# Two of the four weight-block sums of each seven-product pair made by DMA (a plain load and an accumulating load) in place of VectorE adds

## The chip, the cores and the metric

The kernel runs on one core of a Trainium2 chip. A core has a matrix engine (TensorE, PE in the profile, with its weight loads shown apart as PEld), a vector engine (VectorE, DVE), a scalar engine (ScalarE, ACT), a general engine (GpSimd, POOL) and a synchronisation engine (SyncE, SP). Each works through a queue of its own in order. Sixteen DMA engines move data between HBM and the on-chip memory; in this kernel SP issues nearly all transfers. The metric is the device time of one execution in microseconds (us).

## The reference

One step of a one-layer hybrid encoder over T = 544 frames: 32 frames of a running stream and 512 of a new one, model width 1024, all in fp32. The parts that matter here:

```python
xn = _rmsnorm(h, norm_g[l])
proj = xn @ w_in[l]
u, v_m, z_m, ig_pre, fg_pre, q_h, f_h, i_h, g_h, ga, gb = jnp.split(proj, _split_points(), axis=-1)
c, conv_new = _causal_conv(u, conv0, conv_w, conv_b)
c = silu(c)
# mLSTM branch: 4 heads of 512; q and k from c, v from v_m, gate z_m
hm, C_new, n_new, m_new = _mlstm(qm, km, vm, ig, lf, C0, n0, m0)
ya = ((layernorm(hm) + m_skip * c) * silu(z_m)) @ w_brm
# HGRN2 branch: 8 heads of 128, from q_h, f_h, i_h, g_h
oh, S_new = _hgrn(qh, kh, ih, lfh, S0)
yb = (rmsnorm(oh) * silu(g_h)) @ w_brh
y = sigmoid(ga) * ya + sigmoid(gb) * yb
h = h + y @ w_out
h = h + sigmoid(h @ w_pg) * (p @ w_ple)
out = _rmsnorm(h, final_g)
```

The first product, `xn @ w_in`, is the one that the change touches.

## The kernel before, in words

TensorE multiplies in a reduced fp32 form ("fp32r"). To get fp32 results, each operand is split into a high part and a low rest, and each product is made of three matmuls: high x high, high x rest, rest x high. The split of a weight piece (`split_piece`, lines 119 to 130) is a ScalarE copy into the fp32r type for the high half (line 128) and a VectorE subtraction for the low half (line 129). The halves lie in rings of five buffers each (`NPIECE`).

`w_in` is kept in units of 128 output columns; a unit is 128 x 1024 in memory, two pieces of 128 x 512 fp32 (256 KB), so (unit, 0) and (unit, 1) are the two halves of the inner dimension. A raw piece is loaded by a DMA that SP issues (`raw_piece`, lines 116 to 119; line 118 in the profile) into a ring of eight buffers (`NRAW`).

Most units are multiplied plainly (class `One`, matmuls at line 366). 52 units, as 26 pairs (a, b = a + 1), go through class `Two`, which makes the 2 x 2 block product of a pair with seven block products in place of eight. The activations' sums for this are made once for all pairs (`xf_sums`). The weights' sums are made for each pair on VectorE:

```python
s1 = (b,0) + (b,1)
s2 = s1 + (a,0)
s3 = (a,0) + (b,0)
s4 = s2 + (a,1)
```

The seven block products of a pair use the forms a11 = (a,0), s2, a12 = (a,1), s3, s1, a22 = (b,1), s4. Each form is split into halves like a raw piece and multiplied in a block of twelve matmuls of 128 x 272 (line 453). The sums lie in a ring of four buffers (`NSUM`, tag "wu"); the adds are line 418 (tiles named ws1, ws2, ws3, ws4 and the pair's number, all "ws" in a grouped row; wa1180, for example, is form a11 of pair 80, and ws284l the low half of s2 of pair 84).

Class `Pump` (lines 487 to 545) feeds these blocks. It lists all blocks of a stage by start times that are written down in `Two.blocks`: the blocks of two neighbouring pairs are interleaved, seven block times from pair to pair. `prepare` runs three blocks ahead of the one that is multiplied (`AHEAD`): it issues the raw loads, four pieces ahead (`RAWAHEAD`, line 533), and calls the block's `make`, which issues the adds and the split. `make("s2")` made s1 and s2, `make("s3")` made s3, and s4 is made with s2 or a12, whichever comes later.

The 26 pairs are used in two places. In the stages of the mLSTM heads (`fill`, lines 581 to 621), the matmuls of the pairs fill the time between the head's own work: for head 0 pairs 4 and 6, for head 1 pairs 20, 22, 36, 38, 8, 10, for head 2 pairs 24, 26, 40, 42, 12, 14, and for head 3 pairs 28, 30, 44, 46 (the numbers are those of unit a). At the end of the HGRN stage and behind it come the eight gate pairs in the order 80, 88, 82, 90, 84, 92, 86, 94; from about 927 us to 995 us of the span nothing but their blocks is multiplied. Their results pass through gate additions on VectorE (lines 474 and 476) and sigmoids on ScalarE, and then through products with the branch outputs (ya, line 1358).

The order of the instructions on PE is written out by hand. The order on VectorE, ScalarE, POOL and SP in these stages comes from a scheduler, which orders by the order of issue in the program and by the buffers that come free. POOL makes small copies and masks, and issues no DMA.

Of the kernel before, what the change touches and what calls it, by code (L numbers as in the profile page):

```python
# [9 lines left out]
F32 = mybir.dt.float32  # L10
# [4 lines left out]
ALU = mybir.AluOpType  # L15

P = 128
# [22 lines left out]
WP = 512  # L40
NRAW = 8
NSUM = 4
# [20 lines left out]
def hybrid_step(ctx: ExitStack, tc: tile.TileContext, a, o):  # L63
    nc = tc.nc
    V, S, G, PE = nc.vector, nc.scalar, nc.gpsimd, nc.tensor

    cp = ctx.enter_context(tc.tile_pool(name="cp", bufs=1))
    wp = ctx.enter_context(tc.tile_pool(name="wp", bufs=NPIECE))
# [47 lines left out]
    def raw_piece(src, name):  # L116
        raw = wp.tile([P, WP], F32, tag="wr", name=name, bufs=NRAW)
        nc.sync.dma_start(raw[:, : src.shape[-1]], src)
        return raw
# [3 lines left out]
    def split_piece(raw, name, cols=WP, chunk=WP, eng=V):  # L123
        hi = wp.tile([P, WP], F32R, tag="wh", name=name + "h")
        lo = wp.tile([P, WP], F32R, tag="wl", name=name + "l")
        for c in range(0, cols, chunk):
            c = slice(c, min(c + chunk, cols))
            high = S.copy(hi[:, c], raw[:, c])
            low = eng.tensor_tensor(lo[:, c], raw[:, c], hi[:, c].bitcast(F32), ALU.subtract)
        made[name] = high, low  # L130
        return hi, lo

    def weight(src, name, cols=1024, eng=V, chunk=WP):

        raws = [(raw_piece(src[:, c : min(c + WP, cols)], f"{name}r{c}"), min(WP, cols - c)) for c in range(0, cols, WP)]
        return [split_piece(r, f"{name}{i}", n, chunk, eng) for i, (r, n) in enumerate(raws)]
# [71 lines left out]
    def rms_cols(acc, blocks, name, pc=None):  # L208

        pc = pc or paux(name + "pc")  # L210
        n = len(blocks)
        st = small("rms_s", [P, 8])
        V.memset(st[:, :n], 1.0)
        for i, (t0, m) in enumerate(blocks):
            PE.matmul(pc[:m, 0, 2 * i : 2 * i + 2], acc[:, t0 : t0 + m], ones, start=True, stop=True)
        i = 0
        while i < n:
            j = i
            while j < n and blocks[j][1] == blocks[i][1]:
                j += 1  # L220
            m = blocks[i][1]
            V.tensor_scalar(st[:m, i:j], pc[:m, 0, 2 * i : 2 * j : 2], 1.0 / D, EPS, ALU.mult, ALU.add)
            i = j
        r = small("rms_r", [P, 8])
        rsqrt(r[:, :n], st[:, :n], P, n)
        return r
# [77 lines left out]
    def xf_sums(k):  # L304
# [20 lines left out]
        V.scalar_tensor_tensor(l[:, 3], x22, -1.0, h[:, 3].bitcast(F32), ALU.mult, ALU.subtract)  # L325
        return h, l

    xf = [None] * (KD // 2)

    class One:  # L330
# [6 lines left out]
        def raws(self):  # L337
            return [(self.unit, 0), (self.unit, 1)]

        def blocks(self, first):  # L340

            return [
                (i, [(self.unit, i // 2)] if i % 2 == 0 else [], self.prepare(i // 2) if i % 2 == 0 else None, self.run(i), {})
                for i in range(3)
            ] + [(3, [], None, self.run(3), {self.key: 1})]
# [3 lines left out]
        def prepare(self, i):  # L349
            def make(raw):  # L350
                if i == 0:
                    self.w = []
                self.w.append(split_piece(raw[self.unit, i], f"wi{self.unit}{i}"))

            return make
# [27 lines left out]
    class Two:  # L383
# [8 lines left out]

        def raws(self):
            a, b = self.unit, self.unit + 1
            return [(a, 0), (b, 0), (b, 1), (a, 1)]

        def blocks(self, first):
            a, b = self.unit, self.unit + 1
            times = (0, 3, 1, 6, 5, 9, 11) if first else (0, 3, 5, 6, 8, 9, 11)
            k = (self.what, self.f), (self.what, self.f + 1)  # L400
            return [
                (times[0], [(a, 0)], self.make("a11"), self.run("a11", 0, True, self.after1), {}),
                (times[1], [(b, 0), (b, 1)], self.make("s2"), self.run("s2", 0, False, self.after6), {}),
                (times[2], [(a, 1)], self.make("a12"), self.run("a12", 1, True, self.after2), {}),
                (times[3], [], self.make("s3"), self.run("s3", 0, False, self.after7), {}),
                (times[4], [], self.make("s1"), self.run("s1", 1, True, self.after5), {}),
                (times[5], [], self.make("a22"), self.run("a22", 0, False, self.after4), {k[1]: 1}),
                (times[6], [], self.make("s4"), self.run("s4", 1, False, self.after3), {k[0]: 1}),
            ]

        def make(self, form):
            def go(raw):
                a, b = self.unit, self.unit + 1
                q = self.sums

                def add(name, x, y):
                    q[name] = wp.tile([P, WP], F32, tag="wu", name=f"w{name}{a}", bufs=NSUM)
                    V.tensor_tensor(q[name], x, y, ALU.add)

                if form == "s2":  # L420
                    add("s1", raw[b, 0], raw[b, 1])
                    add("s2", q["s1"], raw[a, 0])
                if form == "s3":
                    add("s3", raw[a, 0], raw[b, 0])
                plain_ = {"a11": (a, 0), "a12": (a, 1), "a22": (b, 1)}
                self.w[form] = split_piece(raw[plain_[form]] if form in plain_ else q[form], f"w{form}{a}")
                if form in ("s2", "a12") and "s2" in self.w and "a12" in self.w:
                    add("s4", q["s2"], raw[a, 1])

            return go  # L430
# [77 lines left out]
    class Pump:  # L508
# [18 lines left out]
        def prepare(self, upto):  # L527
            while self.made < min(upto, len(self.order)):
                b = self.order[self.made]
                if b[1]:  # L530
                    need = self.loads.index(b[1][-1]) + 1
                    for u, i in self.loads[self.loaded : need + RAWAHEAD]:
                        self.raw[u, i] = raw_piece(a["w_in"][u][:, i * WP : (i + 1) * WP], f"wi{u}r{i}")
                    self.loaded = max(self.loaded, min(need + RAWAHEAD, len(self.loads)))
                if b[2]:
                    with tc.issue_after(self.behind.ins) if self.behind is not None else nullcontext():
                        b[2](self.raw)
                self.made += 1
# [573 lines left out]
    with tc.manual_schedule(engines={mybir.EngineType.Activation, mybir.EngineType.DVE, mybir.EngineType.PE}):  # L1112
# [15 lines left out]
        for k in range(KD):  # L1128
# [18 lines left out]
            if k in (5, 6):  # L1147
                i, j = ((0, 2), (4, 5))[k - 5]
# [8 lines left out]
        r = rms_cols(sq[0][:, :T], [(0, NS)] + [(NS + b * P, P) for b in range(NB)], "r0", pc)  # L1157
# [410 lines left out]
    for f in range(KD):  # L1568
        w = weight(a["w_brh"][f], f"wbh{f}")
# [10 lines left out]
    for f in range(KD):  # L1580
        t = slot(f"h1{f}")
        nc.sync.dma_start(t[:, :T], a["xT"][f, :, :T])
        w = weight(a["w_out"][f], f"wo{f}")
# [46 lines left out]
    with tc.manual_schedule(engines={mybir.EngineType.PE}):  # L1630
# [6 lines left out]
        for f in range(KD):  # L1637
            pg_unit(1, f)
            if f == 1:
                r = rms_cols(squares[0], blocks, "r10")  # L1640
# [5 lines left out]
        r = rms_cols(squares[1], blocks, "r11")  # L1646
# [93 lines left out]
```

## Time and profile before

| | |
|---|---|
| Time, three runs | 1174.88, 1176.25, 1178.36 us; median 1176.25 |
| The profiled execution's own time | 1176.21 us |
| Its span in the profile | 1174.5 us |
| PE busy | 1160.7 us |
| DVE busy | 883.7 us |
| ACT busy | 615.0 us |
| POOL busy | 142.3 us |
| Read from HBM | 109.32 MB |

How to read it: the span is the time from the first to the last recorded instruction of one execution; the execution's own time has some 1.7 us more around it. The busy time of an engine is the time in which it worked on an instruction; issuing a DMA and waiting don't count. A row of a timeline has the start in us, the duration in us, the engine, the line of the kernel, the operation, the tile written, the tiles read, their shape and type, and how many instructions the row joins; in square brackets stands the idle time just before it and what ended that. In a row of waits stand the waiting engine and line, what it waited for, the total in us, how often, and the longest. In a row of DMA issues the last number is the median time in us from the issue to the landing. A tile's name is shown without its buffer number in grouped rows.

### The profile page before, as it was taken

The page shows a single profiled execution, that of the slowest core. Times are in us where ns is not written, and L with a number is a line of the kernel's source. Part 1 is how long each engine was busy: PE and PEld are TensorE (multiplying, and loading weights), DVE is VectorE, ACT ScalarE, POOL GpSimd, SP SyncE. Part 2 cuts the span into 40 slices and gives each one's busy share as a digit, 9 for nine tenths or more (in the row PEclk, how much of TensorE's full clock was granted, in tenths as well). Part 3 has the DMA queues.
Part 4 walks back from the last instruction along what each step waited for, and adds up shares of the span by engine and source line. Part 5 has one row for each costly group of instructions (what it writes and reads, how often), then busy time and mean ns, then how long its engine had stood idle before and what let it go on. Part 6 is the DMA issues. An engine that isn't in the chain of part 4 may idle for free.

```text
span 1174.5 us, 24294 instructions
## 1 busy us (share of the span) xinstructions
PE 1160.7 (99%) x9089; PEld 1130.7 (96%) x9089; DVE 883.7 (75%) x2156; ACT 615.0 (52%) x1357; POOL 142.3 (12%) x283
## 2 busy tenths in 40 slices
PE   9989999999999999999999999999999999999998
PEld 8989999999999999999999999999999999999998
DVE  6976988576896768967885677877788998654485
ACT  5676557654665556665572343443433666433462
POOL 4933001100111000211000101111101100000000
PEclk9999999999999999999999999999999999999999
DMA  6133315332353233542637222222122273332753
GB/s 230 62 92 121 100 46 165 102 109 100 121 175 119 71 128 113 169 141 98 216 100 243 64 69 63 70 62 71 55 70 63 75 241 99 105 100 77 240 165 113
DMA packets 77902, 135.82 MB, mean 116 GB/s; under 512 B 8788, under 2 KB 16340, under 8 KB 77784
## 3 DMA queue, kind: packets, MB, share of 16 engines
q1 hardware_dynamic: 77616, 134.21, 35.5%
q8 instruction: 71, 1.16, 0.4%
q14 instruction: 47, 0.39, 0.1%
q10 hardware_dynamic: 168, 0.06, 0.0%
HBM read 109.32 MB, written 24.91 MB: 114 GB/s over the span
## 4 chain that ended last, share of the span: by engine, by line
PE 86%; DVE 3%; ACT 1%; issue 1%; ACTq 0%; DVEq 0%
PE d L453 22%; PE d L366 18%; PE ya L149 8%; PE pg L1599 4%; PE yb L149 4%; PE o L149 4%; PE C L833 4%; PE q L149 3%; PE k L149 3%; PE pl L1395 2%; PE nm L1003 2%; PE sc L793 2%; PE ple L149 1%; PE nm L980 1%; PE ht L1461 1%
## 5 line engine op out<-in xcount | busy, mean ns | idle before, releaser
L1387 ACT COPY km<-hk 128x256 f32<-128x256 f32 x56 | 24.0, 429 | 82.1 <-DVE hk L1413 60.1
L569 DVE SCALAR_TENSOR_TENSOR cv<-ub,vec,cv 128x547 f32<-128x547 f32 x48 | 40.4, 842 | 1.3 <-ACT cv L564 0.7
L1395 PE MATMUL pl<-hq,km 128*128 128x128 f32 x224 | 36.0, 284 | 0.0
L1413 DVE TENSOR_TENSOR hq<-hq,q 128x128 f32<-128x128 f32 (+1 forms) x96 | 25.3, 293 | 9.5 <-PE pl L1395 8.4
L933 DVE SCALAR_TENSOR_TENSOR c<-c,wi,Cs 128x258 f32<-128x258 f32 x32 | 15.3, 479 | 21.8 <-PE Cs L931 21.8
L1395 PEld LDWEIGHTS pl<-hq,km 128*128 128x128 f32 x224 | 30.8, 190 | 0.0
L467 ACT COPY t<-d 128x272 f32<-128x272 f32 x78 | 29.5, 378 | 1.2 <-PE d L453 1.0
L1449 POOL TENSOR_TENSOR at<-at,tri 32x32 f32<-32x32 f32 x8 | 3.8, 473 | 208.8 <-DVE at L1420 208.8
L1071 DVE TENSOR_TENSOR y<-ya,y 128x272 f32<-128x272 f32 x48 | 18.9, 436 | 10.7 <-PE ya L149 10.1
L1413 DVE TENSOR_TENSOR hk<-hk,q 128x128 f32<-128x128 f32 x96 | 26.2, 286 | 0.3 <-ACT km L1387 0.2
L845 ACT COPY Co<-C 128x258 f32<-128x258 f32 x32 | 10.4, 378 | 29.2 <-PE C L833 22.4
L1418 DVE COPY_PREDICATED at<-lmask,pl 128x256 f32<-128x256 uint8 x56 | 24.8, 443 | 0.0
L1509 ACT ACTIVATE osq<-kq 128x128 f32<-128x128 f32 x32 | 10.0, 311 | 25.7 <-DVE kq L1503 25.0
L1337 POOL TENSOR_TENSOR kq<-q,hk 128x544 f32<-128x544 f32 x8 | 13.9, 1739 | 61.3 <-DVE q L1335 58.5
L1014 ACT COPY y<-nm 128x516 f32<-128x516 f32 x16 | 9.4, 589 | 21.7 <-PE nm L1003 21.7
L562 POOL COPY uo<-ub 128x3 f32<-128x3 f32 x16 | 11.5, 716 | 71.3 <-DVE ub L474 50.0
L833 PE MATMUL C<-vl,kwh 128*128 128x258 f32 x96 | 19.4, 283 | 0.0
L833 PE MATMUL C<-vh,kwl 128*128 128x258 f32 x96 | 19.4, 284 | 0.0
L833 PE MATMUL C<-vh,kwh 128*128 128x258 f32 x96 | 19.4, 284 | 0.0
L963 DVE BATCH_NORM_STATS2 bs<-y 128x6 f32<-128x512 f32 (+1 forms) x20 | 13.8, 690 | 6.4 <-ACT y L1014 6.2
L731 POOL COPY vsm<-vt 128x96 f32<-128x96 f32 x16 | 7.0, 444 | 87.2 <-ACT vt L478 44.0
L807 ACT CAST sh<-dm 128x512 fp32r<-128x512 f32 (+3 forms) x16 | 7.4, 460 | 19.0 <-DVE dm L801 17.4
(4086 smaller groups left out, 4881.5 us busy)
## 6 DMA issues: line engine op xcount, KB each, us to landing
ya_d<-y SPq DMA_DIRECT2D x32, 272.0 KB, 2.2
y<-ya_d SPq DMA_DIRECT2D x24, 272.0 KB, 4.4
c<-in_C SPq DMA_DIRECT2D x16, 258.0 KB, 3.9
out_Cp<-Co SPq DMA_DIRECT2D x16, 258.0 KB, 2.7
out_Cs<-c SPq DMA_DIRECT2D x16, 258.0 KB, 2.4
x<-in_xT SPq DMA_DIRECT2D x8, 272.5 KB, 4.7
ya<-ya_d SPq DMA_DIRECT2D x8, 272.0 KB, 4.1
h<-in_xT SPq DMA_DIRECT2D x8, 272.0 KB, 4.0
```

The lines of the kernel that those rows point to most:

```text
L149: PE.matmul(both[b][:m, :TH], part(w, off + k * step, m, x), xx[:, half(b)], start=(k == 0 and j == 0), stop=(k == n - 1 and j == 2),)
L366: PE.matmul(self.ps[b][:, : c.stop - c.start], part(self.w, k * P, P, x), xx[:, c], start=(k == 0 and j == 0), stop=(k == KD - 1 and j == 2),)
L453: PE.matmul(ps, ww[:, c], xx, start=(start and k == 0 and j == 0), stop=end, skip_group_check=not start,)
L467: S.copy(t, ps)
L569: V.scalar_tensor_tensor(cv[:, :547], ub[:, j : j + 547], vcol(V_CW + 4 * ft + j), cv[:, :547], ALU.mult, ALU.add)
L793: PE.matmul(pn[:, 0, :n], ks[f][x][:, j * P : (j + 1) * P], qs[f][y][:, NS + j * P : T], start=(f == 0 and i == 0), stop=(f == KH - 1 and ...
L833: PE.matmul(pn[g][:, :VH], kw[b][x][:, f * P : (f + 1) * P], vv[b][y][:, g * VH : (g + 1) * VH], start=(b == 0 and j == 0), stop=(b == NB ...
L1387: S.copy(km.rearrange("p (n j c) -> p n j c", j=2, c=c), view(kk, HB, ((2 * c, NA // (2 * c)), (c - HB, 2), (1, c))),)
L1395: PE.matmul(pn[:, 0, b * P : (b + 1) * P], km[:, b * P : (b + 1) * P], view(qq, b * P, ((2 * c, P // (2 * c)), (HB + c, 2), (1, c))), star ...
L1413: V.tensor_tensor(xv[:, :, i, :], xv[:, :, i, :], t[:, :, 1 - i : 2 - i].to_broadcast([P, m, c]), ALU.mult)
L1418: V.copy_predicated(at[:, :NA], lmask[:, li, :NA], pn[:, 0, :NA])
L1599: PE.matmul(ps, part(w, k * P, P, x), xx[:, c], start=(k == 0 and j == 0), stop=(k == KD - 1 and j == 2))
```

## The change

Of the four sums of each pair, s1 and s3 are no longer added by VectorE. When the pair's first form (a11) is prepared, two sum buffers are taken. Into each of them SP issues a plain load of the piece (b,0); then GpSimd issues a DMA that reads the second piece from HBM, (b,1) for s1 and (a,0) for s3, and adds it to what lies in the buffer (`accum_op=ALU.add`). The piece (b,0) is no longer loaded as a raw piece, since no other form uses it, so a pair has three raw loads in place of four. The sums s2 and s4 stay on VectorE. The order of the blocks on PE is the same.

```diff
+    w_in = a["w_in"]
...
         def raws(self):
             a, b = self.unit, self.unit + 1
-            return [(a, 0), (b, 0), (b, 1), (a, 1)]
+            return [(a, 0), (b, 1), (a, 1)]
...
-                (times[1], [(b, 0), (b, 1)], self.make("s2"), self.run("s2", 0, False, self.after6), {}),
+                (times[1], [(b, 1)], self.make("s2"), self.run("s2", 0, False, self.after6), {}),
...
+                if form == "a11":
+                    for name, u, i in (("s1", b, 1), ("s3", a, 0)):
+                        q[name] = wp.tile([P, WP], F32, tag="wu", name=f"w{name}{a}", bufs=NSUM)
+                        nc.sync.dma_start(q[name], w_in[b][:, :WP])
+                        G.dma_start(q[name], w_in[u][:, i * WP : (i + 1) * WP], accum_op=ALU.add)
                 if form == "s2":
-                    add("s1", raw[b, 0], raw[b, 1])
                     add("s2", q["s1"], raw[a, 0])
-                if form == "s3":
-                    add("s3", raw[a, 0], raw[b, 0])
```

In the changed kernel the lines behind the new ones stand three further down: the plain load of a sum is line 424, the accumulating one 425, the adds 419, the matmuls 456.

More of the change, by code (lines that the diff above doesn't have):

```diff
@@ L532, in prepare @@
                     for u, i in self.loads[self.loaded : need + RAWAHEAD]:
-                        self.raw[u, i] = raw_piece(a["w_in"][u][:, i * WP : (i + 1) * WP], f"wi{u}r{i}")
+                        self.raw[u, i] = raw_piece(w_in[u][:, i * WP : (i + 1) * WP], f"wi{u}r{i}")
                     self.loaded = max(self.loaded, min(need + RAWAHEAD, len(self.loads)))
```

## The prediction

> **What bounds the kernel now.** I read the page first (span, busy times, the chain), then the waits of TensorE, then the windows of the stages that use the changed code.
>
> ```profile
> span 1174.5 us, 24294 instructions
> PE 1160.7 (99%) x9089; PEld 1130.7 (96%) x9089; DVE 883.7 (75%) x2156; ACT 615.0 (52%) x1357; POOL 142.3 (12%) x283
> PE 86%; DVE 3%; ACT 1%; issue 1%; ACTq 0%; DVEq 0%
> ```
>
> PE is busy for 1160.7 of 1174.5 us. All idle time of PE together is 13.8 us, so no relief of another engine can bring more than that. What part of it is VectorE's? The waits of PE, longest first, and the windows around the two places where a weight split is late:
>
> ```profile
> engine line waited for: us in total, times, longest us
> PE d L366 <- ACT wi320h L128: 3.3, 1, 3.3
> PE d L453 <- DVE ws210l L129: 0.4, 1, 0.4
> PE d L453 <- DVE ws214l L129: 0.4, 1, 0.4
> ```
>
> ```profile
> 312.00:334.00 22.00, 21.44 (x163) 20.18 (x162) 20.68 (x41) 14.49 (x31) 5.61 (x7) 1.00 0.43 121
> 463.00:485.00 22.00, 21.45 (x163) 20.18 (x162) 20.63 (x41) 14.43 (x31) 5.61 (x7) 1.00 0.43 129
> 940.00:995.00 55.00, 55.00 (x438) 54.79 (x437) 46.89 (x79) 34.44 (x70) 0.00 (x0) 1.00 0.53 172
> ```
>
> The columns of a window are its length, then PE, PEld, DVE, ACT and POOL busy, the clock, the DMA share and GB/s. Around ws210l and ws214l PE lacks 0.56 and 0.55 us; in the last stretch of pairs (940 to 995) it lacks nothing, DVE works 46.89 of 55 us beside it, and POOL is empty. The chain shows that stretch as one piece of matmuls:
>
> ```profile
> 927.58 12.27 PE d L453 x96
> 940.45 54.37 PE d L453 x431
> ```
>
> Here a pair takes seven blocks of twelve matmuls in 10.55 us (the starts of the same block of two pairs, 945.02 and 955.58 below, are 10.56 apart), and everything that feeds it must keep that pace.
>
> **The change, part by part.** (1) *52 adds leave VectorE.* First and last row of the 26 pairs' adds:
>
> ```profile
> L418 DVE TENSOR_TENSOR ws<-ws,wi4r x2: 687/690/692, 107.5 to 109.9; 128x512 f32<-128x512 f32 x2
> L418 DVE TENSOR_TENSOR ws<-ws,wi88r x2: 683/688/693, 901.0 to 911.3; 128x512 f32<-128x512 f32 x2
> ```
>
> 52 x 0.69 = 35.9 us less of DVE, 883.7 to about 848. On the path lies only what PE waits for: 0.56 + 0.55 us in the two windows and some tenths elsewhere, at most 1.6 us, my estimate. I take 1.0 us of gain, bounds 0 and 1.6.
>
> (2) *Each of those sums becomes a chain.* A plain load goes out on SP into one of the four "wu" buffers, then POOL issues the accumulating load into the same buffer, and only then can VectorE add s2 or ScalarE copy the high half. The chain starts when the buffer is free. In the changed program, s1 of a pair takes the buffer that the s2 of the pair before leaves, and it is free when that pair's s4 has been added. The prices that the trace has:
>
> ```profile
> 924.68 0.33 SPq L118 DMA_DIRECT2D wi90r<-in_w_in  x1
> wi92r<-in_w_in SPq DMA_DIRECT2D x2, 256.0 KB, 3.0
> wi8r<-in_w_in SPq DMA_DIRECT2D x2, 256.0 KB, 2.5
> xh<-kv_d SPq DMA_DIRECT2D x4, 256.0 KB, 6.2
> L1337 POOL TENSOR_TENSOR kq<-q,hk 128x544 f32<-128x544 f32 x8 | 13.9, 1739 | 61.3 <-DVE q L1335 58.5 <-issue 2.8
> L129 POOL TENSOR_TENSOR wk001l<-wk00r,wk001h 128x512 fp32r<-128x512 f32 x1 | 2.4, 2354 | 0.0
> ```
>
> SP issue 0.33 (0.4 with its wake), plain load of 256 KB 3.0 us. No transfer in this trace is issued by POOL and none accumulates, so the second step is bounded: at least the quickest plain load, 2.5 us; at most the slowest transfer of this size, 6.2, behind a POOL instruction of 2.4, 8.6 us. It is nearest to a weight load of 3.0 with one POOL instruction of 1.7 ahead of it and a wake like SP's: I take 5.0. The chain is L = 0.4 + 3.0 + 5.0 = 8.4 us, bounds 5.9 and 12.
>
> A rule bears on the second step. The Trainium skill, "DMA: Bandwidth & Descriptors", section "Anatomy of one DMA — SWDGE (gpsimd) path", fits a GpSimd-issued DMA as 2.0 us plus its bytes at 436 GB/s; for 256 KB that is an estimate of 2.6 us, and L would be 6.0. The section speaks of no accumulation, and no run here shows either; by it neither the tail nor the heads below would lose anything and the sum would be 1175.2 (rival A).
>
> (3) *The tail, 927 to 995 us.* The rows that pace it:
>
> ```profile
> 930.56 0.69 DVE L129 TENSOR_TENSOR ws488l<-ws,ws488h 128x512 fp32r<-128x512 f32 x1 [0.97 <-ACT ws488h L128]
> 936.08 0.69 DVE L129 TENSOR_TENSOR ws182l<-ws,ws182h 128x512 fp32r<-128x512 f32 x1
> 945.01 0.69 DVE L418 TENSOR_TENSOR ws<-ws,wi84r 128x512 f32<-128x512 f32 x1
> 947.43 0.69 DVE L129 TENSOR_TENSOR ws190l<-ws,ws190h 128x512 fp32r<-128x512 f32 x1
> 950.91 0.68 DVE L129 TENSOR_TENSOR ws284l<-ws,ws284h 128x512 fp32r<-128x512 f32 x1
> 959.55 0.68 DVE L129 TENSOR_TENSOR wa2284l<-wi85r,wa2284h 128x512 fp32r<-128x512 f32 x1
> 968.53 0.68 DVE L129 TENSOR_TENSOR ws192l<-ws,ws192h 128x512 fp32r<-128x512 f32 x1
> 978.95 0.69 DVE L129 TENSOR_TENSOR ws186l<-ws,ws186h 128x512 fp32r<-128x512 f32 x1 [0.80 <-ACT ws186h L128]
> 981.96 0.69 DVE L129 TENSOR_TENSOR ws294l<-ws,ws294h 128x512 fp32r<-128x512 f32 x1
> ```
>
> ```profile
> 945.02 0.28 PE L453 MATMUL d<-xfh,ws290h 128*128 128x272 f32 x1
> 955.58 0.28 PE L453 MATMUL d<-xfh,ws284h 128*128 128x272 f32 x1
> 987.24 0.28 PE L453 MATMUL d<-xfh,ws294h 128*128 128x272 f32 x1
> ```
>
> The halves are ready ahead of PE: ws294l ends at 982.65, PE starts it at 987.24, a lead of 4.6 us. Five chains follow one another, each for the next s2. In the changed program's VectorE order, s4 of pair 82 stands right behind ws488l, so it ends at 931.25 + 0.69 = 931.9, and s1 of pair 90 is whole L later, at 940.3, while VectorE reaches its add of s2 behind ws182l, at 936.8: 3.5 us late. VectorE is in order, so the splits and gate additions queued behind that add wait as well, and with them PE, once the lead is gone. Between that add and the end of the next s4 stand, at the pitch of these rows (0.6 for a 512-wide instruction, 0.35 for a 272-wide one, the last in full), 4.7 us of work for pair 90, 4.5 for 84, 2.9 for 92, 4.5 for 86. So s2 of pair 84 can be added at 945.0 + 8.4 = 953.4 (its place behind ws190l is 948.1: 5.3 late), 92 at 966.3 (behind wa2284l, 960.2: 6.1 late), 86 at 977.6 (behind ws192l, 969.2: 8.4 late), 94 at 990.5 (behind ws186l, 979.6: 10.9 late). Less the lead of 4.6, PE stands 6.3 us. In general the loss is 931.9 + 16.6 + 5L - 979.6 - 4.6 = 5L - 35.7: nothing up to L = 7.1, 5 us more for each us of L, 24 us at L = 12. I take 6.3, bounds 0 and 24.
>
> (4) *The head stages.* While a head of the mLSTM branch runs, two pairs follow each other closely only once, in heads 1 to 3 (pairs 36 and 38 of head 1, 40 and 42, 44 and 46):
>
> ```profile
> 245.98 0.68 DVE L129 TENSOR_TENSOR ws420l<-ws,ws420h 128x512 fp32r<-128x512 f32 x1
> 252.83 0.69 DVE L129 TENSOR_TENSOR ws122l<-ws,ws122h 128x512 fp32r<-128x512 f32 x1
> 264.28 0.69 DVE L129 TENSOR_TENSOR ws136l<-ws,ws136h 128x512 fp32r<-128x512 f32 x1 [0.80 <-ACT ws136h L128]
> 272.27 0.68 DVE L919 TENSOR_TENSOR vs<-vts,vs 32x512 fp32r<-32x512 f32 x1
> ```
>
> ```profile
> 276.98 0.28 PE L931 MATMUL Cs<-vs,kws 96*128 96x258 f32 x1
> ```
>
> In the changed order s4 of pair 22 stands behind ws420l and ends at 246.7 + 0.7 = 247.4; s1 of 36 is whole at 255.8, and the add's place is behind ws122l, at 253.5: 2.3 late. By the same count 4.5 us of work end the s4 of 36 at 260.3, s1 of 38 is whole at 268.7, and its add's place is behind ws136l, at 265.0: 3.7 late. What waits behind that add on VectorE and is wanted first is vs (ends at 272.95, PE at 276.98): a lead of 4.0, so nothing is lost at L = 8.4. The lateness is 2L - 13.1: from L = 8.6 on each head loses 2 us per us of L, 2.9 at L = 10, 6.9 at L = 12. I take 0, bounds 0 and 21. The early pairs (80, 88, 20) are loaded long before their use, covered by the HGRN matmuls and the head before; without that cover, one chain of 8.4 each.
>
> (5) *Queues and traffic.* SP issues 26 more (two plain loads for one raw load less), 26 x 0.4 = 10 us spread over the span; a plain load that waits for its buffer holds the raw loads behind it, which are issued some 10 us ahead (wi90r at 924.68, while PE starts on the pair's first sum at 945.02), so I cost it at nothing; uncovered it adds its wait to L. POOL's queue in the tail holds only these transfers. HBM reads rise by 3 x 0.26 MB x 26 = 20 MB; in 940 to 995 that is 0.79 MB per 10.55 us, 75 GB/s on 172, and the DMA share goes in proportion from 0.53 to about 0.76, which is inside the bounds of L.
>
> **Sum:** 6.3 + 0 - 1.0 = 5.3 us on the profiled execution's 1176.21 us (span 1174.5 and 1.7 around it; 0.04 under the median of the runs, 1176.25): 1181.5 us.
>
> **Rivals.** *A, the transfers are hidden.* If the accumulation takes no more than about 4.3 us, L stays under 7.7, the leads take up nearly every delay, and what is left lies between 1176.2 - 1.6 = 1174.6 and 1176.2 + 2.8 - 1.0 = 1178.0 us. For it speak the plain loads of 2.5 to 3.0 us; against it, that each sum needs two transfers one behind the other and POOL's part in the second. 0.22.
>
> *B, an accumulating transfer is far dearer*, 5.8 us or more (it must read its target as well as write it): L from 9.2, where tail and heads give 10.3 + 3.6 - 1.0 = 12.9 us; at L = 10, 14.3 + 8.7 - 1.0 = 22.0; at L = 12, 44: 1189 to 1220 us. For it speaks the 6.2 us row; against it, most weight loads at 3. 0.24.
>
> *C, POOL in order.* In the heads, POOL holds back its own work and the accumulations behind it:
>
> ```profile
> POOL vs L916 <- PE Cs L931: 94.3, 3, 34.6
> ```
>
> If accumulations that PE needs soon stand behind that wait, or small casts for PE behind an accumulation that waits for its plain load, each of three heads loses up to one L: up to 25 us, 1185 to 1207. Against it: POOL's 142.3 us of work leave it free most of the time, and a longer wait for Cs ends before the next pairs are due. 0.06.
>
> *D, the other side: VectorE's relief wins.* The late splits ws210l and ws214l and gate additions come earlier, and L stays under 7.1. It decides only where more than 3.5 us of PE's 13.8 us of idling hang on VectorE's adds; the rows above show at most 1.6. 1172. 0.05.
>
> **How the numbers follow.** The forecast, L between 7.7 and 9.2, has 0.43; its own range is 1178 to 1189, its value 1181.5. About 0.3% (3.5 us) is what a measurement of this kernel can tell from no change. Same: A's 0.22 and 0.08 of the forecast's lower end (to 1179.7). Faster: D, 0.05. Slower: 0.35 + 0.24 + 0.06 = 0.65. The range, 1175 to 1203, leaves out D, A's lowest part and the last part of B and C, about 0.18 in all.
>
> **What would show it.** Right: DVE near 848 us; PE below 55 of 55 us between 940 and its end, with waits of PE for ws2 and ws1 splits of pairs 86 and 94; VectorE idle ahead of its remaining adds, released by a POOL transfer, growing from pair 90 to 94. L can be read as the time from the plain load's issue to that add. Wrong: POOL transfers that land within 4.3 us and a full PE (A); gaps all over the heads (B or C); a gap that another engine releases.

## The result, and the profile after

| | before | after |
|---|---|---|
| Time, median of the runs | 1177.09 us (1174.88 to 1178.36) | 1213.78 us (1211.34 to 1216.3) |
| Ratio, with its 95% interval | | 1.0315 (1.0301 to 1.0328) |
| Span of the profiled execution | 1174.5 us | 1212.2 us |
| Mean granted clock over the span | 0.999 | 0.986 |

The changed kernel is 3.1% slower, about 37 us. The page of the changed kernel, first the span and the busy times, then the DMA queues and the HBM traffic, then the shares of the chain that ended last:

```profile
span 1212.2 us, 24512 instructions
PE 1172.9 (97%) x9089; PEld 1141.9 (94%) x9089; DVE 850.1 (70%) x2104; ACT 616.1 (51%) x1357; POOL 181.4 (15%) x335
...
q0 software_dynamic: 7488, 13.63, 7.2%
...
HBM read 129.77 MB, written 24.91 MB: 128 GB/s over the span
PE 84%; DVE 7%; DMA 5%; issue 2%; ACT 2%; SPq 0%; POOL 0%; DVEq 0%; ACTq 0%; POOLq 0%
```

VectorE fell from 883.7 to 850.1 us as worked out, and reads rose to 129.77 MB as worked out. But the span grew by 37.7 us, and it grew in two ways. PE's idle time went from 13.8 to 1212.2 - 1172.9 = 39.3 us (25.5 more). And the same 9089 matmuls took 1172.9 us in place of 1160.7 (12.2 more). In the chain, DMA, absent before, has 5%. (On POOL the page counts the issuing of the 52 DMAs as busy time, 45.7 of its 181.4 us.)

Where did it come from? I took the start of the same matmul in both traces; the difference is the lag at that point. The matmuls are named by their weight half:

| the same matmul | start before | lag after | since the row above |
|---|---|---|---|
| wi331h, before the heads | 116.58 | 1.9 | 1.9 |
| ws410l, end of head 1 | 332.22 | 8.3 | 6.3 |
| ws414l, end of head 2 | 483.60 | 14.1 | 5.8 |
| ws246h, end of head 3 | 589.50 | 22.3 | 8.2 |
| ws388h, start of the gate stretch | 927.51 | 23.8 | 1.6 |
| ws494h, behind the gate stretch | 996.29 | 36.9 | 13.1 |

So the heads 1 to 3 lose, some 6 to 8 us each, and the last stretch of gate pairs loses 13.1 us. The waits of the changed kernel, PE's longest, and then what VectorE waited for:

```profile
PE vt L903 <- DVE vt L477: 13.0, 3, 5.5
PE d L456 <- DVE gb L477: 7.4, 2, 4.6
...
PE d L456 <- DVE ga L477: 1.1, 1, 1.1
PE d L456 <- ACT ws210h L128: 1.1, 1, 1.1
PE d L456 <- ACT ws214h L128: 1.1, 1, 1.1
```

```profile
DVE ws L419 <- DMA ws<-in_w_in: 46.6, 13, 7.2
```

PE names VectorE, but VectorE is not busy: it stands 46.6 us in 13 places before the add of s2 until the sum's transfer has landed. What PE is short of is not weights but additions on VectorE (vt in the heads, the gate additions gb and ga in the last stretch), which stand behind that add. The waits of ws210 and ws214 did not shrink; they are 1.1 us where they were 0.4.

One link of the last stretch, in order (timeline rows of SP, POOL, DVE and PE of the changed kernel, put one under the other):

```profile
968.54 0.33 SPq L424 DMA_DIRECT2D ws<-in_w_in  x1
...
973.14 0.86 POOL L425 DMA_DIRECT2D ws<-in_w_in  x1 [10.84 <-ACT wa2290h L128]
...
979.12 0.69 DVE L419 TENSOR_TENSOR ws<-ws,wi84r 128x512 f32<-128x512 f32 x1 [7.18 <-DMA ws<-in_w_in]
...
980.68 0.43 DVE L477 TENSOR_TENSOR gb<-d,t 128x272 f32<-128x272 f32 x1
...
981.17 0.60 PE L456 MATMUL d<-xfh,ws190h 128*128 128x272 f32 x1 [4.62 <-DVE gb L477]
```

This is the sum s1 of pair 84. The plain load starts at 968.54, GpSimd issues the second transfer at 973.14, the add of s2 can start at 979.12: L is 10.6 us. VectorE idles 7.18 us ahead of the add, and the gate addition gb, three instructions behind it, lets PE go on at 981.17, after 4.62 us of idling. The windows of the stretch, from the start of ws388h to that of ws494h, and around this gap (columns as in the prediction):

```profile
951.34:1033.23 81.89, 73.38 (x547) 72.54 (x547) 51.85 (x104) 43.52 (x95) 8.59 (x10) 0.94 0.66 172
975.00:980.00 5.00, 1.55 (x13) 1.32 (x11) 0.88 (x2) 0.00 (x0) 0.87 (x1) 0.95 0.97 253
980.00:985.00 5.00, 3.83 (x17) 3.83 (x18) 4.96 (x10) 3.96 (x9) 0.00 (x0) 0.50 0.59 170
985.00:990.00 5.00, 5.00 (x37) 5.00 (x37) 2.96 (x6) 3.32 (x7) 0.89 (x2) 0.86 0.85 224
```

PE lacks 81.89 - 73.38 = 8.5 us here where it lacked nothing. Behind the gap the granted clock is 0.50 for some five us of work: 3.83 us of PE time from 980 to 985 are 17 matmuls, while 5.00 us from 985 to 990 are 37. This is the second part of the loss, and no stall shows it.

A head, the same way (head 1, pair 38; its VectorE and PE rows, then the windows around them):

```profile
272.07 0.69 DVE L419 TENSOR_TENSOR ws<-ws,wi38r 128x512 f32<-128x512 f32 x1 [5.17 <-DMA ws<-in_w_in]
272.68 0.43 DVE L477 TENSOR_TENSOR vt<-d,t 128x272 f32<-128x272 f32 x1
...
273.17 0.69 PE L903 MATMUL vt<-ident,vt 128*128 128x128 f32 x2 [3.87 <-DVE vt L477]
```

```profile
262.00:268.00 6.00, 6.00 (x51) 6.00 (x50) 4.00 (x7) 3.06 (x6) 0.21 (x1) 1.00 0.89 290
268.00:272.00 4.00, 1.30 (x12) 1.07 (x9) 0.00 (x0) 0.59 (x1) 2.69 (x10) 1.00 0.66 84
272.00:275.00 3.00, 1.83 (x8) 1.83 (x9) 2.93 (x6) 1.21 (x2) 0.00 (x0) 0.66 0.67 147
```

VectorE has no work at all from 268 to 272; 5.17 us of its waiting become 3.87 us of PE's, and the clock falls after that too (0.66).

### The profile page after: what moved, and what is told of

Read it like the earlier page. It is cut to its first block, busy times and chain, and to the rows that moved or that the text cites. A ratio compares the mean times of both kernels' runs of the same rounds, so it can differ in the third digit from the quotient of the medians.

```text
span 1212.2 us, 24512 instructions
## 1 busy us (share of the span) xinstructions
PE 1172.9 (97%) x9089; PEld 1141.9 (94%) x9089; DVE 850.1 (70%) x2104; ACT 616.1 (51%) x1357; POOL 181.4 (15%) x335
## 3 DMA queue, kind: packets, MB, share of 16 engines
q0 software_dynamic: 7488, 13.63, 7.2%
HBM read 129.77 MB, written 24.91 MB: 128 GB/s over the span
## 4 chain that ended last, share of the span: by engine, by line
PE 84%; DVE 7%; DMA 5%; issue 2%; ACT 2%; SPq 0%; POOL 0%; DVEq 0%; ACTq 0%; POOLq 0%
PE d L367 19%; PE d L456 17%; PE ya L149 8%; PE q L149 4%; PE pg L1602 4%; PE yb L149 4%; DMA ws<-in_w_in 4%; PE k L149 4%; PE o L149 4%; PE C L836 4%; PE sc L796 3%; PE pl L1398 2%; PE nm L1006 2%; PE u L269 1%; DVE cv L572 1%
## 5 line engine op out<-in xcount | busy, mean ns | idle before, releaser
L425 POOL DMA_DIRECT2D ws<-in_w_in x52 | 45.7, 879 | 244.8 <-DMA ws<-in_w_in 42.8
L903 PE MATMUL vt<-ident,vt 128*128 128x128 f32 x64 | 12.5, 318 | 13.2 <-DVE vt L477 13.0
L1512 ACT ACTIVATE osq<-kq 128x128 f32<-128x128 f32 x32 | 10.0, 311 | 26.2 <-DVE kq L1506 25.5
L753 DVE TENSOR_TENSOR kl<-kf,kh 128x512 fp32r<-128x512 f32 x16 | 11.1, 692 | 17.1 <-ACT kh L752 16.0
L903 PEld LDWEIGHTS vt<-ident,vt 128*128 128x128 f32 x64 | 8.8, 160 | 14.3 <-DVE vt L477 13.7
L1340 POOL TENSOR_TENSOR kq<-q,hk 128x544 f32<-128x544 f32 x8 | 13.9, 1742 | 45.7 <-DVE q L1338 42.9
L564 POOL COPY uo<-ub 128x3 f32<-128x3 f32 x16 | 15.3, 958 | 30.5 <-DVE ub L479 16.1
```

What stands on the lines that cost most here:

```text
L425: G.dma_start(q[name], w_in[u][:, i * WP : (i + 1) * WP], accum_op=ALU.add)
```

## The experiments

In each table row of waits or windows the line numbers are those of that kernel; all ratios are against the kernel before. The lags are read as above, at the same six matmuls. Three questions were open: is it the price of the accumulating transfer, is it the moment at which the chain may start (its buffer), or is it the added traffic?

**e1: more sum buffers in the shared ring.** The ring of sums gets six buffers, and the raw ring gives two up for the room.

```diff
-NRAW = 8
-NSUM = 4
+NRAW = 6
+NSUM = 6
```

> The changed kernel with six sum buffers in place of four, and six raw buffers in place of eight (a pair now loads three raw pieces, so two pairs still fit; the memory is the same). Theory 'start': a chain of plain load and accumulating load (7.9 to 10.7 us, read in the changed kernel's tail from the end of the s4 add to the s2 add) starts only when the s4 add of the pair before frees its buffer, VectorE waits for it in order, and PE waits for what stands behind. With two buffers more s1 and s3 of the next pair can be loaded about a pair earlier, and the waits vanish: 1176 to 1182 us, TensorE clock back at 1.00 in the tail. Rival 'traffic': 20 MB more from HBM and accumulations that take twice the engine time per MB (7.2% of 16 engines' span for 13.63 MB against 35.9% for 141.03) slow every load; the same transfers are made here, so 1205 to 1214 us.

Measured: 1214.11 us, ratio 1.0314 (1.0289 to 1.034): no gain at all. The lags are 0.0, 9.2, 17.6, 24.8, 24.2, 36.7. This seemed to speak against the start. But the number of buffers is not the time for which one is free: the sums go round one shared ring, and in this program's order the plain load for s1 of pair 84 takes the buffer of s1 of pair 82, which is free only after the split ws182l (it ends at 961.55, and the load goes out at 961.57). The experiment changed which buffer the chain waits for, and not enough how early it may begin. It decided nothing, and e5, e6 and e9 take the question up again with rings of their own.

**e2: only s1 by two transfers.** s3 goes back to VectorE, with its raw piece.

```diff
-for name, u, i in (("s1", b, 1), ("s3", a, 0)):
+for name, u, i in (("s1", b, 1),):
...
+if form == "s3":
+    add("s3", raw[a, 0], raw[b, 0])
```

> Only s1 is made by the two DMAs; s3 is again a VectorE add of (a,0) and (b,0), which is loaded as a raw piece again. Theory 'start': s1 stands on the path to s2, so nearly the whole loss stays: 1203 to 1214 us, perhaps a little less than the changed kernel since the chain shares the DMA engines with one accumulation fewer. Rival 'traffic': half of the added transfers are gone, so half of the loss: about 1195 us.

**e3: only s3 by two transfers.** The counterpart, with the add of s1 back on VectorE.

```diff
-for name, u, i in (("s1", b, 1), ("s3", a, 0)):
+for name, u, i in (("s3", a, 0),):
...
+add("s1", raw[b, 0], raw[b, 1])
```

> Only s3 is made by the two DMAs; s1 is again a VectorE add. Theory 'start': s3 is first needed three blocks (4.5 us) after s2 and nothing but its own split waits for it, so most of the loss goes: 1177 to 1186 us. Rival 'traffic': half of the added transfers are left, about 1195 us.

Measured: e2 1241.85 us, ratio 1.0544 (1.0522 to 1.0566); e3 1179.02 us, ratio 1.0015 (1.0003 to 1.0027). Each has half of the added traffic and half of GpSimd's transfers; one loses more than the whole change, and more than was expected by either theory; the other loses next to nothing. So neither the traffic nor the number of transfers sets the loss: it is s1, which another sum, s2, is waiting for. In e3 VectorE idles before no add for a sum's transfer (for raw pieces it waits up to 3.1 us). e2's lags are 2.1, 20.6, 40.1, 48.7, 50.7, 64.7: the gate stretch costs 14.0 us as in the change, but heads 1 and 2 cost 18 and 19. There another chain is late as well (DVE timeline, then PE's waits, of e2):

```profile
328.00 0.69 DVE L419 TENSOR_TENSOR ws<-ws,wi10r 128x512 f32<-128x512 f32 x1 [5.32 <-DMA ws<-in_w_in]
```

```profile
PE vt L905 <- DVE vl L909: 12.3, 3, 6.2
PE yt L1050 <- DVE c L1057: 8.7, 2, 5.0
```

At 328.00 it is pair 10's add that stands on VectorE ahead of work for the head's output (c, line 1057), which PE waits for. The sums take the shared ring in another order here, one early in place of two; why just this chain became late I did not follow further.

**e4: the second transfer without accumulation.** GpSimd's transfer overwrites the buffer; the sums s1 and s3 then hold the second piece only.

```diff
-G.dma_start(q[name], w_in[u][:, i * WP : (i + 1) * WP], accum_op=ALU.add)
+G.dma_start(q[name], w_in[u][:, i * WP : (i + 1) * WP])
```

> The DMA that GpSimd issues overwrites the buffer in place of adding to it (so s1 and s3 hold the second piece alone and the output is not the reference's); every queue, wait and byte read from HBM stays. If the accumulation itself is dear, the second step falls from 4.6 us to about 3.5 and the chain from 9.2 to about 8: by the prediction's slope (5 us in the tail and about 6 in three heads for each us) 1200 to 1205 us. If the price lies in two transfers one behind the other and in GpSimd's issue, the time stays at 1209 to 1214 us.

Measured: 1195.75 us, ratio 1.0153 (1.013 to 1.0175), lags 1.1, 4.0, 6.7, 10.5, 11.2, 19.7. The group of GpSimd's issues and its queue, of the change and then of e4 (busy us and mean ns; packets, MB, share of 16 engines' span):

```profile
L425 POOL DMA_DIRECT2D ws<-in_w_in x52 | 45.7, 879 | 244.8 <-DMA ws<-in_w_in 42.8
```

```profile
L425 POOL DMA_DIRECT2D ws<-in_w_in x52 | 28.5, 549 | 239.7 <-DMA ws<-in_w_in 36.0
...
q0 software_dynamic: 4160, 13.63, 3.7%
```

For the same 13.63 MB, the accumulating queue had 7488 packets and 7.2% of 1212.2 us on the engines, the plain one 4160 and 3.7% of 1195.1: 87 against 44 us, twice as much. In the gate stretch of e4 GpSimd's transfer lands in 3.4 us (median), against 4.6 in the same stretch of the change. The accumulation is thus worth 1213.78 - 1195.75 = 18.0 us of the 37. The time is below the 1200 to 1205 us expected of a dear accumulation. The other half, 18 us, stays when the second transfer is a plain one: it belongs to the chain of two transfers that starts late, as e8 and e9 bear out.

**e5: three buffers for s1, and every sum a ring of its own.** The same number of transfers, the accumulation stays; the raw ring shrinks to five.

```diff
-NRAW = 8
-NSUM = 4
+NRAW = 5
+NSUM = {"s1": 3, "s2": 1, "s3": 2, "s4": 1}
...
-tag="wu", bufs=NSUM
+tag=f"wu{name}", bufs=NSUM[name]
```

> The changed kernel, with a ring of its own for each sum: three buffers for s1, two for s3, one each for s2 and s4, and five raw buffers in place of eight (the same memory). All transfers and their bytes stay. In its program the load of s1 of pair 94 waits for the split of s1 of pair 84, three pairs back, some 21 us ahead of the add of s2 in the pace of the kernel before; a chain of 8 to 11 us fits. Theory 'start' (what counts is when the chain may begin): 1175 to 1183 us, the waits of VectorE for these transfers gone. Rival 'traffic' (added bytes and dear accumulation slow the loads themselves, which six shared buffers didn't mend): 1200 us or more. Five raw buffers hold 1.7 pairs; if that is too few, VectorE or ScalarE wait for wi pieces instead.

**e6: two buffers for s1.** The same edit with `{"s1": 2, "s2": 1, "s3": 2, "s4": 1}` and NRAW = 6.

> As the run before with two buffers for s1 in place of three, and six raw buffers. The load of s1 of pair 94 now waits for the split of s1 of pair 92, two pairs of the alternating order nearer. In the pace of the kernel before, the split of s1 ends 13.5 us after the add of s2 of its pair (945.0 to 958.5), so 21.1 - 13.5 = 7.6 us are left for a chain of 8 to 11: theory 'start' expects most of the loss to be back, 1195 to 1214 us. Rival 'traffic': the same time as with three buffers.

Measured: e5 1198.51 us, ratio 1.0171 (1.0153 to 1.019); e6 1201.55 us, ratio 1.0204 (1.0184 to 1.0224). e5 is above the 1175 to 1183 us expected of an early start. By their totals they look alike; by their lags they are opposites:

| since the row above | change | e5 | e6 |
|---|---|---|---|
| up to wi331h | 1.9 | 11.1 | -0.1 |
| head 1 | 6.3 | -0.6 | 1.0 |
| head 2 | 5.8 | -0.9 | 3.1 |
| head 3 | 8.2 | 0.7 | 5.7 |
| up to the gate stretch | 1.6 | 12.3 | -0.6 |
| gate stretch | 13.1 | 0.0 | 14.8 |

With three s1 buffers the places that the change had spoiled lose nothing. What e5 lost, it lost elsewhere, at about 73 to 99 and 612 to 635 us, where other weights come through the raw ring that had been cut to five (PE's waits of e5 that the change does not have):

```profile
PE ya L149 <- ACT wbm301h L128: 2.4, 1, 2.4
...
PE q L149 <- ACT wq001h L128: 2.1, 1, 2.1
```

With two buffers the gate stretch loses as much as in the change. Its reason, in e6's rows (DVE, SP, DVE):

```profile
990.58 0.68 DVE L129 TENSOR_TENSOR ws192l<-ws,ws192h 128x512 fp32r<-128x512 f32 x1
...
991.29 0.33 SPq L424 DMA_DIRECT2D ws<-in_w_in  x1
...
1000.16 0.69 DVE L419 TENSOR_TENSOR ws<-ws,wi94r 128x512 f32<-128x512 f32 x1 [1.88 <-DMA ws<-in_w_in]
```

The plain load for s1 of pair 94 goes out at 991.29, as soon as the split of s1 of pair 92 ends at 991.26, and its add comes 8.9 us later: the wait for the buffer is the start of the chain.

**e7: a late VectorE alone.** The kernel before, with one add of s2 of pair 84 repeated fourteen times: a stall of VectorE without any transfer.

```diff
 add("s2", q["s1"], raw[a, 0])
+if a == 84:
+    for _ in range(14):
+        V.tensor_tensor(q["s2"], q["s1"], raw[a, 0], ALU.add)
```

> The kernel before, with the add of s2 of pair 84 made 14 times more (the same result each time): 14 x 0.69 = 9.7 us of VectorE in the tail, and no DMA changed. It measures what one stall of VectorE costs: PE has leads of about 4.6 us, so it should stand some 5 us. Theory 'clock' (an idle gap of PE by itself lowers the granted TensorE clock for some us, as the windows behind the gaps of the changed kernel show with 0.50 to 0.86): about 2 us more than the gap, 1183 to 1187 us, and a clock under 1.00 in the 5 us behind the gap. If the clock falls for another reason (the added transfers): the gap alone, 1181 to 1183 us, at 1.00.

Measured: 1185.61 us, ratio 1.0069 (1.0048 to 1.0089). The PE row at the gap and the windows behind it, of e7:

```profile
961.59 0.59 PE L456 MATMUL d<-xfh,ws284h 128*128 128x272 f32 x1 [5.90 <-ACT ws284h L128]
```

```profile
960.00:965.00 5.00, 3.42 (x14) 3.19 (x15) 4.85 (x9) 2.56 (x5) 0.00 (x0) 0.50 0.10 22
965.00:970.00 5.00, 5.00 (x36) 5.00 (x36) 4.34 (x9) 2.88 (x6) 0.00 (x0) 0.86 0.40 140
970.00:975.00 5.00, 5.00 (x42) 5.00 (x41) 4.77 (x8) 2.76 (x6) 0.00 (x0) 1.00 0.55 176
```

PE idles 5.90 us; the lag is 6.0 us at that matmul and 8.4 us ten us later, and stays there. The 2.4 us between are paid in clock: 0.50, then 0.86, then 1.00, and the DMA share is 0.10 where the clock is lowest, so it is not the transfers that slow PE. An idle gap of this size costs 1.4 times its length.

**e8: the plain load alone.** GpSimd's transfer is left out, so s1 and s3 hold the piece (b,0) only.

```diff
-G.dma_start(q[name], w_in[u][:, i * WP : (i + 1) * WP], accum_op=ALU.add)
```

> The changed kernel without the accumulating DMAs: s1 and s3 hold the piece (b,0) alone (so the output is not the reference's), the chain is SP's issue and one plain load, 3.1 us by the changed kernel's row, and VectorE stays relieved of its 52 adds. By the prediction's slope a chain of 3.5 us costs nothing: 1174.5 to 1178 us, which also bounds what the relief of VectorE is worth (1.6 us at most by the prediction). If the plain loads' waits in SP's queue cost time by themselves: 1180 us or more.

Measured: 1175.82 us, ratio 0.999 (0.998 to 1.0). VectorE has 854.1 us of work and waits for no sum any more: one transfer fits. This is what relieving VectorE of 52 adds is worth, with the rest of the change free: 0 to 0.2%.

**e9: three buffers for s1, and a raw ring of six.** As e5, with `{"s1": 3, "s2": 1, "s3": 1, "s4": 1}` and NRAW = 6. It computes all that the change computes.

> As the run with three s1 buffers, but with six raw buffers in place of five and one s3 buffer in place of two (the same memory). There the pair stages lost nothing any more (against the kernel before, PE's lag was 10.7 us at pair 10 of head 1 and 10.4 at the end of head 3, 22.7 at the start and the end of the tail), and what was lost lay at 73 to 99 us and 612 to 635 us, where weights of other products go through the raw ring. If five raw buffers were the cause, those 22 us go, as they did with six raw buffers in the two runs that had them: 1177 to 1184 us. The one s3 buffer leaves 9.3 us per pair for a chain of 8 to 11 us: where that is too little, some us come back in the tail, up to 1190. If the 22 us had another cause (the added transfers), 1198 us.

Measured: 1176.96 us, ratio 1.0 (0.9989 to 1.001). The page, and the windows of head 1 and of the gate stretch, of e9:

```profile
span 1175.8 us, 24448 instructions
PE 1162.5 (99%) x9089; PEld 1133.2 (96%) x9089; DVE 853.7 (73%) x2104; ACT 615.1 (52%) x1357; POOL 185.4 (16%) x335
...
q0 software_dynamic: 7488, 13.63, 7.3%
...
HBM read 129.77 MB, written 24.91 MB: 132 GB/s over the span
```

```profile
225.00:290.00 65.00, 65.00 (x517) 64.28 (x516) 42.09 (x75) 34.69 (x74) 12.45 (x28) 1.00 0.49 131
940.00:995.00 55.00, 54.45 (x432) 54.03 (x431) 40.58 (x70) 33.94 (x69) 6.03 (x7) 1.00 0.74 205
```

The same transfers, the same accumulation at the same price (7.3% of the engines), the same 129.77 MB; and PE is full again in head 1 and lacks 0.55 us in the gate stretch, at a clock of 1.00. Rows of e9 say why three buffers do and two don't:

```profile
943.52 0.69 DVE L419 TENSOR_TENSOR ws<-ws,wi84r 128x512 f32<-128x512 f32 x1
...
958.56 0.69 DVE L129 TENSOR_TENSOR ws184l<-ws,ws184h 128x512 fp32r<-128x512 f32 x1 [0.72 <-ACT ws184h L128]
...
976.15 0.69 DVE L419 TENSOR_TENSOR ws<-ws,wi94r 128x512 f32<-128x512 f32 x1
```

The buffer of s1 of pair 84 is needed from the add at 943.52 until the split ends at 959.25, 15.7 us. Pairs follow every 10.56 us. Two buffers leave a chain 2 x 10.56 - 15.7 = 5.4 us, less than any chain measured; three leave 16.0 us, more than any. The add for pair 94 at 976.15 has no idle time before it, where the same add in the change waited 2.22 us and those before it up to 7.18.

No version beats both kernels: with the late start gone, e9 stands at 1.000, and e8 bounds what the relief can give.

## Why the prediction was wrong, step by step

The direction and its mechanism were right: the chain of two transfers is late for the add of s2, VectorE stands in order behind it, and PE goes short. The size was too small by 32 us, for three reasons, in the order of their size (part of the clock's share lies in the heads).

**Step (4), the heads: the failing step.** The sentence that fails is that what waits behind that add and is wanted first is vs, with "a lead of 4.0, so nothing is lost". It is vt, the gate addition that stands right behind the add. These are its rows in the kernel before (DVE, PE):

```profile
265.62 0.43 DVE L474 TENSOR_TENSOR vt<-d,t 128x272 f32<-128x272 f32 x1
...
266.94 0.60 PE L900 MATMUL vt<-ident,vt 128*128 128x128 f32 x4
```

vt ended at 266.05 and PE took it at 266.94, a lead of 0.9; from the changed trace, 5.17 - 3.87 = 1.3 us. So the threshold was not L = 8.6 but, with a lead of 1.3, L = 7.2. By the prediction's own lateness of 2L - 13.1, a head loses 3.7 - 1.3 = 2.4 us even at the forecast L of 8.4. And L was longer here. s4 of pair 36 ended at 262.14 and s2 of 38 could be added at 272.07: 9.9 us. The plain load's part was 5.6 us (SP issued it at 262.21, GpSimd the second transfer at 267.79), not 3.4, in a window with a DMA share of 0.89: loads of the head's state (c) were in flight, which the sum did not look at. The three heads cost 20.3 us in place of 0: 15.0 of idling, 13.0 of them in PE's waits for vt, and 5.3 of slower matmuls.

**The clock: a term that the sum didn't have.** PE's busy time grew by 12.2 us with the same matmuls: 5.3 us in the heads, 4.6 in the gate stretch, and 2.1 in the first 110 us. e7 shows the mechanism by itself for a gap of 5.90 us. After gaps of 3.87 and 4.62 us the windows show it in the change. After a shorter gap, of 1.08 us, the clock stayed at 1.00, and after one of 2.80 us, which ended at 1008.98, it fell (PE row of the first, then a window for each, of the change):

```profile
995.39 0.37 PE L456 MATMUL d<-xfh,ws184h 128*128 128x272 f32 x1 [1.08 <-DVE ga L477]
```

```profile
995.00:1000.00 5.00, 4.61 (x37) 4.64 (x38) 4.47 (x8) 4.10 (x9) 0.00 (x0) 1.00 0.74 232
1010.00:1015.00 5.00, 5.00 (x31) 5.00 (x30) 3.06 (x6) 1.96 (x4) 0.79 (x1) 0.66 0.48 157
```

The Trainium skill, "TensorE: Matmul & The Clock Gate", section "Part 1: The HAM clock gate (the "warmup" mystery)", states that TensorE falls to half clock after an idle window of about 3.4 us and returns to full after about 3.4 us of work, and that the window runs freely. The rows agree on 0.50 after 4.62 and 5.90 us and on nothing after 1.08. But the clock also fell behind the gap of 2.80 us, and behind the one of 4.62 it stayed at 0.50 for some five us of work; the measurement decides. The prediction had its gaps worked out to 6.3 us and could have asked what one such gap costs. The kernel before held an answer: PE waits 3.28 us for wi320h and starts at 67.67, and behind that the clock is low. The window there, of the kernel before and of the changed one:

```profile
70.00:80.00 10.00, 10.00 (x74) 10.00 (x74) 8.54 (x18) 7.54 (x15) 2.51 (x3) 0.90 0.44 137
70.00:80.00 10.00, 10.00 (x64) 10.00 (x63) 8.66 (x19) 6.29 (x11) 1.38 (x2) 0.75 0.42 133
```

The 1.9 us of the first 110 us are clock too: 0.75 in place of 0.90 here, behind the same gap (3.27 us), and 0.89 in place of 1.00 between 100 and 110, though PE's longest gap just ahead of that is 0.7 us in both. e9 lost 1.95 us there at nearly the same clocks (0.76 and 0.89); e1 lost nothing, at 0.89 and 1.00. All have the changed transfers, so these do not explain it; why the clock fell further in one execution than in another stays open.

**Step (2), L: mis-sized in two of five links.** Forecast 8.4. The five chains of the gate stretch, from the plain load's issue to the add of s2, took 8.3, 10.6, 10.5, 8.4 and 7.8 us, 9.1 in the mean (9.2 from the end of the s4 before). GpSimd's transfers took 4.6 us in the median from issue to landing, 3.7 to 7.1, and some 0.7 us between the plain load's landing and GpSimd's issue come on top; the 5.0 taken was near, and the lower bound of 2.5 far. The two long links, of pairs 84 and 92, ran beside SP's loads of ya, p and h: the DMA share while they were under way was 0.95 and 0.88, against 0.62 to 0.68 in the other three. In e4 the same two are the long ones (10.9 and 9.6 us at 0.84 and 0.79, the other three 6.7 to 7.0), so the accumulation is not what sets them apart. That the other loads do is read from these windows; no run takes them away. The estimate of 2.6 us from the Trainium skill ("DMA: Bandwidth & Descriptors", section "Anatomy of one DMA — SWDGE (gpsimd) path") isn't met by the accumulating transfer, nor by the median of the plain ones from GpSimd of e4 (3.2; the quickest 2.7); the measurement decides. Rival A, which hung on at most 4.3 us, was near for single transfers and wrong for the chain.

**Step (3), the gate stretch: right in its chain, near in its size, wrong in the place.** Each of the five plain loads went out within 0.1 us of the end of the s4 before, as worked out. The formula 5L - 35.7 with the measured L (46 us for five chains with their starts) gives 10.2; PE idled 8.5. In e4, with 41.6 us, it gives 5.9; e4's PE lacks 77.30 - 71.30 = 6.0 in its stretch:

```profile
938.67:1015.97 77.30, 71.30 (x546) 70.24 (x546) 52.03 (x104) 43.48 (x95) 5.38 (x10) 0.98 0.58 182
```

But PE was to stand for the splits of pairs 86 and 94, with VectorE's waits growing from pair 90 to 94. These waits were 2.5, 7.2, 3.2, 4.5 and 2.2 us, and PE stood for the gate additions behind the adds of pairs 84 (4.6), 92 (1.1) and 86 (2.8): the short leads that step (4) missed. The lead of 4.6 that the formula takes off was not the one that counted, so that it came this near is in part luck. Off besides were L, and the 4.6 us of clock.

**Step (1), the relief: right in VectorE's time, nothing in the kernel's.** 850.1 us against about 848. The 1.0 us of gain can't be seen in the time; e8 and e9 put it at 0.2% at most. In e9's trace the lag does fall over heads 1 and 2, where ws210l and ws214l were late, from 1.95 to 0.5 us. **Step (5), queues and traffic: right in the bytes, too even in the share.** 129.77 MB against 109.3 + 20; e9 carries all of it, at 0.74 of the DMA engines in the gate stretch (0.76 worked out), without loss. In the change the share was not even, as the two long links under step (2) show.

**The rivals.** B gave 1189 to 1220 us, which holds 1213.8, but not by its condition: at the measured mean L of 9.1 to 9.2 its formulas give no more than 1189. Its cause, the dear accumulation, is 18 of the 37 us (e4). The other half is the chain's start. And the accumulation's price loses everything only because of that start: in e9 it is paid in full and costs nothing. C and D found nothing: no wait of PE for a late GpSimd cast is among the longest, and VectorE's relief is worth at most 0.2%.

The loss by stage, between the matmuls of the table of lags (us, PE's time in the two traces):

| stage | longer by | PE idle, more | PE busy, more |
|---|---|---|---|
| up to wi331h | 1.9 | -0.1 | 2.1 |
| heads 1 to 3 | 20.3 | 15.0 | 5.3 |
| up to the gate stretch | 1.6 | 1.4 | 0.1 |
| gate stretch | 13.1 | 8.5 | 4.6 |
| behind it | 0.8 | 0.8 | 0.0 |

The 1.4 us ahead of the gate stretch are waits for tf in the HGRN stage. The 2.0 us of idling in the heads beside vt hold longer waits for the splits of ws210 and ws214 and other small ones.

## What to carry to other kernels

A load in two steps, one transfer that must land before the other is issued, needs its buffer free for the whole length of both before the use: work that time out from who releases that very buffer, pair by pair, not from the number of buffers. Where an instruction in an in-order queue becomes late, list everything that stands behind it in that stage and take the shortest lead, not the lead of the work that it feeds. And price a gap of TensorE with its clock: behind gaps of 2.80 to 5.90 us it added some four tenths of the idle time (2.4 us on 5.9 in e7, 9.9 on 23.5 in the heads and the gate stretch of the change).

## What the hardware showed that I had not expected

An accumulating DMA from HBM takes twice the time on the DMA engines of a plain one of the same bytes from the same queue (87 against 44 us for 13.63 MB, with 7488 packets against 4160), and GpSimd is busy 0.88 us with issuing one, against 0.55. From issue to landing it is 4.6 us against 3.2 for 256 KB (medians of 52, the change and e4).

A gap of 5.90 us of TensorE cost 8.4 us (e7), with no transfer changed. Behind a gap of 2.80 us the clock fell as well; behind one of 1.08 us it did not.
